# Three more seven-product quads in a fused attention and state-space block

## The chip, the cores and the metric

The kernel runs on one core of a Trainium2 chip. The metric is the device time of one execution in microseconds; the time given for a kernel is the median of its runs. One further execution is taken by the hardware profiler: its views are the page, groups of instructions, waits, the chain of waits that ended last, the order of time, and stretches (windows) with the busy time of every engine.

## The reference

One layer of a hybrid block on x of 256 rows and 2048 columns, all in float32:

```
proj = rms_norm(x) @ w_in            # q, k, v, z_a, z_s, xbc, dt, g_a, g_s
o_a  = dilated attention of q, k, v (16 heads, three patterns mixed) * silu(z_a)
y    = rms_norm(chunked state-space scan of xbc, dt * silu(z_s))
merged = sigmoid(g_a) * (o_a @ w_attn_branch) + sigmoid(g_s) * (y @ w_ssm_branch)
out  = rms_norm(x + merged @ w_out)
```

With 256 rows nearly all work is weight matrices streaming past a small x. The weights hold some 481 units of 128 x 1024 numbers (512 KB each).

## The kernel before, in words

**Units and their split.** A weight unit is loaded on SP's DMA queue into a ring of five buffers (`w`). ScalarE writes its high part `h` (line 278), VectorE the rest `l = w - h` (line 279), and TensorE multiplies with three matmuls of 512 columns each: x's high part with h and with l, x's low part with h (lines 484 to 486, in `triple`). That is how float32 accuracy is had from the faster matmul format. `h` and `l` have four buffers each.

**Passes.** The second half of the program runs in this order: state-space branch (`ssm`, two passes of 16 quads), value projection (`v`, two passes), 16 heads (`q`, `k`, `za` and the attention itself), attention gate (`ga`, two passes, units 385 and 401 on), attention branch (`attn`, units 417 and 433 on), output (`out`, units 449 and 465 on). A pass (function `gemm_pair`) makes 256 x 1024 outputs out of quads. A quad is two units of weights: two k blocks by two column blocks. It is done in one of two ways:

- plain: 2 k blocks x 2 row halves x 2 column halves, a `triple` each: 24 matmuls. VectorE and ScalarE split two units.
- seven-product (Strassen's scheme): seven triples, 21 matmuls. It needs sums of the weights: `t` (its sum made earlier and spilled to DRAM in `sum_jobs`, or made on the spot) and `u` (line 565), and sums of x (`sx`, made in `keep_left`, spilled, fetched back by `fetch_left`). VectorE makes `la`, `lc`, `ltt`, `ltu` and line 565, ScalarE `ha`, `hc`, `htt`, `htu`. `htt/ltt` and `htu/ltu` take two buffer pairs (`ht`, `lt`); the value passes have two pairs more.

`S_QUADS` lists the seven-product quads of each pass, `V_ORDERS`, `G_ORDERS`, `A_ORDERS` the order in which a pass takes its eight quads. After a pass, `fold` adds four product banks (two ScalarE copies, lines 589 and 590, and VectorE lines 591 to 594), then the element-wise sums follow (1018 for the gate, 1155 for the attention branch) and, for the attention branch, the merge with the gates (1144, 1145). The merged blocks are then transposed on TensorE (`turn_m`, line 1137, banks `mtp`). The two passes of a pair use the PSUM banks in swapped roles.

**What sets the order.** The order of quads and the hooks that start loads (`behind_unit`: a one-column GpSimd copy that waits for a unit's split, and a DMA on SP behind it) are written by hand. Between them a list scheduler places instructions on every engine; the splits of weights go ahead of other work by `L_AHEAD`. Each engine runs its own list strictly in order. Hooks sit on plain quads' units alone.

**Places.** `cst` holds in columns 0 to 384 the causal mask of the scan, then the identity, `ones` and `sel`; `cw` the convolution's weights. The attention's tables (distances and counts, 768 columns) have had a tile of their own, `dc`, in pool `xl`, loaded behind unit 274. Pool `xk` holds one `sx` tile, `xl` three, `vx` (in the value passes) one for quad 3.

Of the kernel before, what the change touches and what calls it, by code (L numbers as in the profile page):

```python
# [9 lines left out]
F32 = mybir.dt.float32  # L10
F32R = mybir.dt.float32r
# [4 lines left out]
P = 128  # L16
# [48 lines left out]
SUM_UNITS = 2, 9, 16  # L65
LEFT_EVERY, ATT_EVERY = 11, 4
SUM_LAG = 3
# [131 lines left out]
def hybrid_block(ctx: ExitStack, tc: tile.TileContext, wall, xt, x, pk_d, cst_d, fw_d, out):  # L199
# [34 lines left out]
    def behind_unit(n, f):  # L234
        on_unit.setdefault(n, []).append(f)
# [56 lines left out]
    def blocks(t, c):  # L292
        return [t[:, i, (c + j) * 512 : (c + j + 1) * 512] for i in range(2) for j in range(2)]
# [143 lines left out]
    def fetch_left(kept, pool, bufs, key, x, spare, u):  # L437
        def get(behind):
            sx = new_sx(pool, bufs, spare, f"{key[0]}{key[1]}")
            gp.tensor_copy(sx[:, 0, 0, 0:1], behind)  # L440
            nc.sync.dma_start(sx.bitcast(F32), lefts[key])
            kept[key[1]] = left_parts(sx, x, spare)

        behind_unit(u, get)
# [156 lines left out]
    def rsqrt_rows(sums, n, name):  # L601
        var = lead.tile([P, 2], F32, name=f"var_{name}", tag="var", bufs=1)
        ve.tensor_scalar(var, sums, 1.0 / n, EPS, ALU.mult, ALU.add)
        r = lead.tile([P, 2], F32, name=f"r_{name}", tag="rr", bufs=1)
        gp.tensor_tensor(r, var, half, ALU.pow)
        hr = lead.tile([P, 2], F32, name=f"hr_{name}", tag="hr", bufs=1)
        ve.tensor_scalar(hr, r, 0.5, None, ALU.mult)
        return r, hr
# [84 lines left out]
    with tc.tile_pool(name="ssm", bufs=2) as sp:  # L693
# [223 lines left out]

        for n, q in enumerate(SX_X + SX_V):
            behind_unit(begin + 3 + n * LEFT_EVERY, lambda behind, q=q: left_x(q, behind))
# [108 lines left out]
    with tc.tile_pool(name="vx", bufs=1) as vx:  # L1028
        tl = big.tile([P, 4, UNIT], F32R, name="tl_v", tag="yo0b")
        room["tl"] = [(tl[:, 2 * n], tl[:, 2 * n + 1]) for n in range(2)]  # L1030
        for n, q in enumerate(SX_V):
            fetch_left(sx_of_x, vx, len(SX_V), ("x", q), two_kts(XT, q), 0, FIRST[("v", 0)])
        for n, q in enumerate(SX_X[1:]):
            fetch_left(sx_of_x, xl, len(SX_X) - 1, ("x", q), two_kts(XT, q), 0, FIRST[("v", 0)] + 1 + n)
        for c in (0, 2):
            es, prods = gemm_pair(
                ("v", c), lambda kt: XT[:, kt, :], KT, sx_of_x, c == 2, order=V_ORDERS[c], room=room
            )
            dst = blocks(vt, c)
            fold(prods, dst)  # L1040
            for d, e in zip(dst, es):
                ve.tensor_tensor(d, e, d, ALU.add)
    sx_of_o = {}

    with tc.tile_pool(name="att", bufs=2) as ap:
# [4 lines left out]
        def scores(h, q, k, p):  # L1050
# [4 lines left out]
            slope = 2.0 ** (-8.0 * (h + 1) / NH)  # L1055
            ve.scalar_tensor_tensor(t, dist_c, slope / SCALE, sps[:, :384], ALU.mult, ALU.add)
            st = ap.tile([P, 8], F32, name=f"st{h}", tag="st", bufs=1)
# [6 lines left out]
            for i, (a, b) in enumerate(parts):  # L1064
                ve.scalar_tensor_tensor(
                    p[:, a:b], p[:, a:b], 1.0, count_c[:, a:b], ALU.mult, ALU.mult,
                    accum_out=st[:, 4 + i : 5 + i],
                )
# [10 lines left out]
        def mix(h, pT, za):  # L1079
# [13 lines left out]
        sum_jobs(  # L1093
            SUMS_ATT, range(FIRST[("q", 0)] + 7, N_UNITS, ATT_EVERY),
            [
# [188 lines left out]
```

## Time and profile before

| | us |
|---|---|
| median of 3 runs (lowest, highest) | 1381.28 (1380.21, 1382.47) |
| the profiled execution, in all | 1381.59 |
| its span, first to last instruction | 1379.8 |
| TensorE busy, VectorE busy, ScalarE busy, GpSimd busy | 1368.4, 1168.4, 836.6, 142.5 |

The span leaves out 1.8 us around the instructions. In the order of time a row is: start, duration, engine, line, operation, tile written <- tiles read, shape, count; what stands in brackets is idle time ahead of it and who ended it. A group's row has, behind the bar, busy time and mean of one, and behind the next bar the idle time ahead of it with its releasers. Tile names in the trace come without their numbers.

### The profile page before, as it was taken

To read this page: it belongs to the slowest core of one execution; us is meant where nothing else is said; L and a number is where in the kernel's file an instruction comes from. 1 tells how busy PE (TensorE), PEld (TensorE's weight loads), DVE (VectorE), ACT (ScalarE), POOL (GpSimd) and SP (SyncE) were. 2 spreads that over 40 slices of the span, in tenths; PEclk is the share of its full clock that TensorE was granted. 3 is DMA by queue.
4 is the path that set the end of the run, shared out by engine and by line. 5 is a ranking of instruction groups with operands and counts; after the bars stand their busy time and mean duration, and the time that the engine had idled before them with its cause. 6 is when DMAs were issued, how large, how long until landed. Compare 5 with 4: busy or idle time off the path is not lost.

```text
span 1379.8 us, 20706 instructions
## 1 busy us (share of the span) xinstructions
PE 1368.4 (99%) x7266; PEld 1166.4 (85%) x7266; DVE 1168.4 (85%) x1753; ACT 836.6 (61%) x1306; POOL 142.5 (10%) x226
## 2 busy tenths in 40 slices
PE   9999999999999999999999999999999999999997
PEld 7888888888888888888888888888888888888886
DVE  6897999897899898788989887777877788888997
ACT  7655777675667676666565554454445556655554
POOL 2301111101010100010001001211111000000112
PEclk9999999999999999999999999999999999999999
DMA  9766978778787867578677668888888757875773
GB/s 348 232 193 198 334 261 284 263 245 283 249 278 236 302 200 223 175 240 277 228 259 273 209 218 282 280 275 276 289 288 300 241 163 268 290 224 177 247 271 122
DMA packets 105080, 345.00 MB, mean 250 GB/s; under 512 B 11728, under 2 KB 13712, under 8 KB 104976
## 3 DMA queue, kind: packets, MB, share of 16 engines
q1 hardware_dynamic: 103536, 339.62, 73.7%
q10 hardware_dynamic: 1440, 4.06, 0.8%
q8 instruction: 57, 0.93, 0.3%
q14 instruction: 47, 0.39, 0.1%
HBM read 314.87 MB, written 28.77 MB: 249 GB/s over the span
## 4 chain that ended last, share of the span: by engine, by line
PE 95%; DMA 2%; ACT 1%; issue 1%; DVE 1%; SPq 0%; POOL 0%; POOLq 0%; ACTq 0%; DVEq 0%
PE ps_xs L333 8%; PE ps_zs L333 8%; PE ps_za L333 4%; PE ps_k L333 4%; PE ps_q L333 4%; PE ps_xs L339 4%; PE ps_zs L339 4%; PE ps_ssm L485 3%; PE ps_ssm L486 3%; PE ps_ssm L484 3%; PE ps_q L339 2%; PE ps_k L339 2%; PE ps_za L339 2%; PE ps_gs L421 2%; PE ps_gs L422 2%; PE ps_gs L420 2%
## 5 line engine op out<-in xcount | busy, mean ns | idle before, releaser
L278 ACT ACTIVATE h<-w 128x1024 fp32r<-128x1024 f32 (+1 forms) x398 | 413.8, 1047 | 303.9 <-issue 80.9
L279 DVE TENSOR_TENSOR l<-w,h 128x1024 fp32r<-128x1024 f32 (+1 forms) x398 | 478.8, 1209 | 114.0 <-ACT h L278 110.4
L333 PE MATMUL ps_zs<-XT,h 128*128 128x512 f32 x496 | 172.1, 393 | 0.0
L333 PE MATMUL ps_xs<-XT,h 128*128 128x512 f32 x496 | 171.6, 393 | 0.0
L339 PE MATMUL ps_zs<-XT,l 128*128 128x256 f32 x496 | 134.8, 280 | 0.9 <-DVE l L279 0.9
L339 PE MATMUL ps_xs<-XT,l 128*128 128x256 f32 x496 | 133.7, 277 | 0.0
L333 PEld LDWEIGHTS ps_xs<-XT,h 128*128 128x128 f32 x496 | 91.3, 188 | 19.4
L333 PEld LDWEIGHTS ps_zs<-XT,h 128*128 128x128 f32 x496 | 91.3, 188 | 18.8
L339 PEld LDWEIGHTS ps_zs<-XT,l 128*128 128x128 f32 x496 | 93.3, 188 | 3.7 <-DVE l L279 1.6
L339 PEld LDWEIGHTS ps_xs<-XT,l 128*128 128x128 f32 x496 | 93.2, 188 | 2.1
L333 PE MATMUL ps_q<-XT,h 128*128 128x512 f32 x256 | 91.1, 404 | 0.0
L333 PE MATMUL ps_k<-XT,h 128*128 128x512 f32 x256 | 88.6, 395 | 0.0
L333 PE MATMUL ps_za<-XT,h 128*128 128x512 f32 x256 | 88.4, 394 | 0.0
L551 ACT ACTIVATE ha<-wa 128x1024 fp32r<-128x1024 f32 x43 | 45.4, 1055 | 43.6 <-PE ps_ssm L486 12.9
L339 PE MATMUL ps_q<-XT,l 128*128 128x256 f32 x256 | 68.4, 278 | 0.0
L339 PE MATMUL ps_k<-XT,l 128*128 128x256 f32 x256 | 68.4, 277 | 0.0
L339 PE MATMUL ps_za<-XT,l 128*128 128x256 f32 x256 | 68.4, 277 | 0.0
L792 ACT ACTIVATE gt<-acb,acT 128x128 f32<-128x128 f32 x128 | 44.0, 391 | 28.8 <-DMA acb<-acum_d 27.4
L552 DVE TENSOR_TENSOR la<-wa,ha 128x1024 fp32r<-128x1024 f32 x43 | 52.4, 1219 | 9.3 <-ACT ha L551 9.2
L552 DVE TENSOR_TENSOR ltu<-wa,htu 128x1024 fp32r<-128x1024 f32 x38 | 46.3, 1219 | 15.9 <-ACT htu L551 15.9
L333 PEld LDWEIGHTS ps_k<-XT,h 128*128 128x128 f32 x256 | 47.0, 188 | 9.9
L333 PEld LDWEIGHTS ps_q<-XT,h 128*128 128x128 f32 x256 | 47.1, 188 | 9.7
(688 smaller groups left out, 3315.1 us busy)
## 6 DMA issues: line engine op xcount, KB each, us to landing
w<-in_wall SPq DMA_DIRECT2D x394, 512.0 KB, 4.8
wa<-in_wall SPq DMA_DIRECT2D x43, 512.0 KB, 5.1
th_a<-in_wall SPq DMA_DIRECT2D x19, 512.0 KB, 5.6
sums_at<-in_wall SPq DMA_DIRECT2D x18, 512.0 KB, 4.7
acb<-acum_d SPq DMA_DIRECT2D x32, 256.0 KB, 3.8
t_ssm<-sums_at SPq DMA_DIRECT2D x13, 512.0 KB, 4.8
wt<-t_ssm SPq DMA_DIRECT2D x13, 512.0 KB, 4.7
th_a<-in_wall SPq DMA_DIRECT2D x19, 256.0 KB, 6.2
```

What stands on the lines that cost most here:

```text
L278: ac.activation(h[:, a:b], w[:, a:b], AF.Copy)
L279: ve.tensor_tensor(l[:, a:b], w[:, a:b], h[:, a:b].bitcast(F32), ALU.subtract)
L333: high = pe.matmul(acc, h[:, kk, :], xs_of(kt), start=(kt == 0), stop=False)
L339: low = pe.matmul(acc[:, S:], l[:, kk, :], xs_of(kt)[:, :S], start=False, stop=(kt == KT - 1))
L420: pe.matmul(accs[i], xh, h[:, kk], start=(kt == 0), stop=False)
L421: pe.matmul(accs[i], xh, l[:, kk], start=False, stop=False)
L484: pe.matmul(acc, xh, h, start=start, stop=False)
L485: pe.matmul(acc, xh, l, start=False, stop=False)
L486: pe.matmul(acc, xl, h, start=False, stop=stop)
L551: ac.activation(h, src, AF.Copy)
L552: ve.tensor_tensor(l, src, h.bitcast(F32), ALU.subtract)
L792: ac.activation(g4[:, n, b], acb[:, j, b // 2 * P : b // 2 * P + P], AF.Relu, scale=-1.0, bias=sc[:, h : h + 1],)
```

## The change

Quad 3 becomes a seven-product quad in both gate passes, and quad 5 in the first attention pass. The gate's order takes quad 4 ahead of quad 1, so that plain quads are 0, 1 and 7; the first attention pass takes 5 ahead of 6. The left sums of x for quad 3, so far used in the first value pass alone, are kept through the gate: `xl` has four tiles, and `vx` goes. To make room, `dc` goes: the distances are loaded over the mask, the counts over `cw` and over `ones` and `sel`, by three loads. `rsqrt_rows` takes one tile instead of three. The sums to be made under the heads are 22 instead of 19, 3.75 units apart instead of 4, from the third unit on instead of the seventh.

```
-A_ORDERS = {0: (0, 1, 2, 4, 3, 6, 5, 7), 2: (0, 2, 1, 4, 3, 5, 6, 7)}
+A_ORDERS = {0: (0, 1, 2, 4, 3, 5, 6, 7), 2: (0, 2, 1, 4, 3, 5, 6, 7)}
-G_ORDERS = {c: (0, 2, 1, 4, 3, 5, 6, 7) for c in (0, 2)}
+G_ORDERS = {c: (0, 2, 4, 1, 3, 5, 6, 7) for c in (0, 2)}
...
-    ("v", 0): (2, 3, 4, 5, 6), ("v", 2): (2, 4, 5, 6), ("ga", 0): (2, 4, 5, 6), ("ga", 2): (2, 4, 5, 6),
-    ("attn", 0): (2, 4, 6), ("attn", 2): (2, 4, 5, 6), ("out", 0): (3, 5), ("out", 2): (3, 5),
+    ("v", 0): (2, 3, 4, 5, 6), ("v", 2): (2, 4, 5, 6), ("ga", 0): (2, 3, 4, 5, 6), ("ga", 2): (2, 3, 4, 5, 6),
+    ("attn", 0): (2, 4, 5, 6), ("attn", 2): (2, 4, 5, 6), ("out", 0): (3, 5), ("out", 2): (3, 5),
...
-SX_X = (2, 4, 5, 6)
-SX_V = (3,)
-O_BEHIND = 7, 14, 15, 17
+SX_X = (2, 4, 3, 5, 6)
+O_BEHIND = 3, 14, 15, 17
...
-    dc = xl.tile([P, 768], F32, name="dc", tag="dc")
-    dist_c, count_c = dc[:, :384], dc[:, 384:]
-    behind_unit(FIRST[("v", 2)] + 1, lambda behind: fetch(dc, cst_d[:, :768], behind))
+    count = lead.tile([P, P], F32, name="count", tag="cw"), cst[:, 512:768]
+    for n, (dst, a) in enumerate(((mask3, 0), (count[0], 384), (count[1], 512))):
+        behind_unit(FIRST[("v", 2)] + n, lambda behind, dst=dst, a=a: fetch(dst, cst_d[:, a : a + dst.shape[-1]], behind))
...
-            SUMS_ATT, range(FIRST[("q", 0)] + 7, N_UNITS, ATT_EVERY),
+            SUMS_ATT, [FIRST[("q", 0)] + 3 + n * 15 // 4 for n in range(len(SUMS_ATT))],
```

Lines of the changed kernel are one lower up to about line 600, two lower in the state-space part and five lower from the attention on. TensorE's list is nine matmuls shorter. What moves on VectorE is shown at two places; the first number in a tile's name is the weight unit (a seven-product quad goes by its first unit), the second only tells instances apart.

The first place is VectorE in the first gate pass, where the last head's attention ends (p15, oaTb and sxt_o6 are its leftovers; units 385 to 388 are quads 0 and 1, 389 and 393 are quads 2 and 4). Before:

```order
L1071 TENSOR_SCALAR p15_11472<-p15_11472,st15_11557 128x256
L279 TENSOR_TENSOR l387_11671<-w387_11668,h387_11670 128x1024
L288 TENSOR_TENSOR oaTb_10571<-za14_11294,oaTb_10571 128x256
L288 TENSOR_TENSOR sxt_o6_11537<-sxt_o6_11537 128x512
L279 TENSOR_TENSOR l388_11677<-w388_11674,h388_11676 128x1024
L552 TENSOR_TENSOR la393_11710<-wa393_11704,ha393_11709 128x1024
L552 TENSOR_TENSOR lc393_11714<-wc393_11706,hc393_11713 128x512
L565 TENSOR_TENSOR wa393_11704<-wa393_11704,th_a_7806 128x1024
L552 TENSOR_TENSOR ltu389_11638<-wa389_11619,htu389_11637 128x1024
```

The same place in the changed kernel:

```order
L1066 TENSOR_SCALAR p15_11495<-p15_11495,st15_11580 128x256
L551 TENSOR_TENSOR la393_11697<-wa393_11691,ha393_11696 128x1024
L287 TENSOR_TENSOR oaTb_10585<-za14_11317,oaTb_10585 128x256
L287 TENSOR_TENSOR sxt_o6_11560<-sxt_o6_11560 128x512
L564 TENSOR_TENSOR wa393_11691<-wa393_11691,th_a_7802 128x1024
L551 TENSOR_TENSOR lc393_11701<-wc393_11693,hc393_11700 128x512
L278 TENSOR_TENSOR l387_11737<-w387_11734,h387_11736 128x1024
L278 TENSOR_TENSOR l388_11743<-w388_11740,h388_11742 128x1024
L551 TENSOR_TENSOR ltu389_11661<-wa389_11642,htu389_11660 128x1024
```

Quad 4's la, lc and line 565's operation (now 564) have moved ahead of quad 1's two units.

The second place is VectorE at the end of attention pass 0 and the start of pass 2 (units 431 and 432 are quad 7 of pass 0, 429 its quad 6, 433 to 436 quads 0 and 1 of pass 2, 437 its quad 2; fin takes the fold, th_a and th_s the merge). Before:

```order
L279 TENSOR_TENSOR l431_12555<-w431_12552,h431_12554 128x1024
L279 TENSOR_TENSOR l432_12561<-w432_12558,h432_12560 128x1024
L592 TENSOR_TENSOR fin_12270<-pp_attn0_3_12353,fin_12270 128x512
L552 TENSOR_TENSOR ltt437_12693<-fin_12270,htt437_12692 128x1024
L593 TENSOR_TENSOR fin_12270<-fin_12270 128x512
L279 TENSOR_TENSOR l433_12642<-w433_12639,h433_12641 128x1024
L594 TENSOR_TENSOR fin_12270<-fin_12270 128x512
L279 TENSOR_TENSOR l434_12648<-w434_12645,h434_12647 128x1024
L1155 TENSOR_TENSOR fin_12270<-ps_attn0_0_12271,fin_12270 128x512
L1155 TENSOR_TENSOR fin_12270<-ps_attn0_1_12272,fin_12270 128x512
```

After them come, up to unit 435's l, 10 more operations of 512 columns, la437, line 565's on wa437, and lc437. The same place in the changed kernel:

```order
L278 TENSOR_TENSOR l432_12604<-w432_12601,h432_12603 128x1024
L551 TENSOR_TENSOR ltt429_12567<-fin_12307,htt429_12566 128x1024
L278 TENSOR_TENSOR l433_12685<-w433_12682,h433_12684 128x1024
L551 TENSOR_TENSOR ltu429_12571<-wa429_12553,htu429_12570 128x1024
L278 TENSOR_TENSOR l434_12691<-w434_12688,h434_12690 128x1024
L590 TENSOR_TENSOR fin_12307<-pp_attn0_2_12389,fin_12307 128x512
L1150 TENSOR_TENSOR fin_12307<-ps_attn0_0_12308,fin_12307 128x512
L591 TENSOR_TENSOR fin_12307<-pp_attn0_3_12390,fin_12307 128x512
L551 TENSOR_TENSOR ltt437_12736<-fin_12307,htt437_12735 128x1024
L1139 SCALAR_TENSOR_TENSOR th_a_7802<-th_a_7802,fin_12307 128x512
L592 TENSOR_TENSOR fin_12307<-fin_12307 128x512
L551 TENSOR_TENSOR la437_12727<-wa437_12722,ha437_12726 128x1024
```

Quad 6's ltt and ltu and all of the fold now stand behind unit 432's l; some of the merge has moved behind unit 435's l. Then follow 1140, 593, 1150, 564 on wa437, lc437, 1150 twice, 1139 and unit 435's l.

More of the change, by code (lines that the diff above doesn't have):

```diff
@@ L65 @@
 SUM_UNITS = 2, 9, 16
-LEFT_EVERY, ATT_EVERY = 11, 4
+LEFT_EVERY = 11
 SUM_LAG = 3
@@ L1023, in hybrid_block @@
     xl = ctx.enter_context(tc.tile_pool(name="xl", bufs=1))
[L1024 to L1026 removed]
+    count = lead.tile([P, P], F32, name="count", tag="cw"), cst[:, 512:768]
+    for n, (dst, a) in enumerate(((mask3, 0), (count[0], 384), (count[1], 512))):
+        behind_unit(FIRST[("v", 2)] + n, lambda behind, dst=dst, a=a: fetch(dst, cst_d[:, a : a + dst.shape[-1]], behind))
     room = room_of(big.tile([P, 6 * 512], F32, name="room_v", tag="yo0a"), 2, 2)
[L1028 to L1042, printed above, removed]
+    tl = big.tile([P, 4, UNIT], F32R, name="tl_v", tag="yo0b")
+    room["tl"] = [(tl[:, 2 * n], tl[:, 2 * n + 1]) for n in range(2)]
+    for n, q in enumerate(SX_X[1:]):
+        fetch_left(sx_of_x, xl, len(SX_X) - 1, ("x", q), two_kts(XT, q), 0, FIRST[("v", 0)] + n)
+    for c in (0, 2):
+        es, prods = gemm_pair(
+            ("v", c), lambda kt: XT[:, kt, :], KT, sx_of_x, c == 2, order=V_ORDERS[c], room=room
+        )
+        dst = blocks(vt, c)
+        fold(prods, dst)
+        for d, e in zip(dst, es):
+            ve.tensor_tensor(d, e, d, ALU.add)
     sx_of_o = {}
```

11 lines of the change are left out of this document (5 added, 6 removed).

## The prediction

> **What bounds the kernel now.** I read the page first, then the chain of waits, then stretches cut at the passes, then the order of time around the passes that change. From the page (40 slices of 34.5 us, busy tenths, and the granted TensorE clock):
>
> ```profile
> span 1379.8 us, 20706 instructions
> PE 1368.4 (99%) x7266; PEld 1166.4 (85%) x7266; DVE 1168.4 (85%) x1753; ACT 836.6 (61%) x1306; POOL 142.5 (10%) x226
> PE   9999999999999999999999999999999999999997
> PEclk9999999999999999999999999999999999999999
> PE 95%; DMA 2%; ACT 1%; issue 1%; DVE 1%; SPq 0%; POOL 0%; POOLq 0%; ACTq 0%; DVEq 0%
> ```
>
> TensorE sets the end: 95% of the chain is its work, and its clock is granted in full in every slice. A busy share alone does not prove that matmuls stand as close as they can, so the pitch comes next. Two rows of TensorE in the order of time, at the change from attention pass 0 to pass 2 (start, duration):
>
> ```profile
> 1242.38 0.39 PE L484 MATMUL ps_attn<-h,oaTa 128*128 128x512 f32 x1
> 1244.42 0.39 PE L484 MATMUL ps_attn<-h,oaTa 128*128 128x512 f32 x1
> ```
>
> The first and the tenth of ten matmuls in a row: nine steps in 2.04 us, 0.227 us each, although one lasts 0.39 (they overlap). Now the passes (PE, weight load, VectorE, ScalarE, GpSimd busy, clock, DMA share): the two value passes, the two gate passes, the two attention passes.
>
> ```profile
> 745.00:787.00 42.00, 42.00 (x187) 34.75 (x187) 37.98 (x41) 24.09 (x28) 3.29 (x3) 1.00 0.71 247
> 787.00:829.00 42.00, 42.00 (x191) 34.88 (x189) 38.30 (x41) 23.32 (x26) 0.00 (x0) 1.00 0.58 193
> 822.00:1117.00 295.00, 295.00 (x1719) 259.10 (x1718) 222.50 (x419) 146.03 (x224) 43.83 (x57) 1.00 0.81 273
> 1117.00:1159.00 42.00, 42.00 (x191) 34.76 (x190) 35.28 (x52) 25.64 (x33) 0.00 (x0) 1.00 0.68 221
> 1159.00:1201.00 42.00, 42.00 (x188) 34.84 (x187) 37.66 (x41) 27.14 (x33) 2.12 (x4) 1.00 0.82 289
> 1201.00:1243.00 42.00, 42.00 (x187) 34.80 (x186) 36.30 (x41) 24.20 (x28) 0.00 (x0) 1.00 0.73 230
> 1243.00:1286.00 43.00, 43.00 (x199) 35.63 (x199) 38.30 (x48) 24.26 (x31) 3.16 (x1) 1.00 0.58 186
> ```
>
> TensorE never waits in any of them: 187 matmuls in 42 us is the same 0.225 us pitch. So a matmul taken out is worth its pitch, and any wait that the change makes is paid in full. The runner-up is VectorE, with 4.3 to 6.7 us to spare in each pass that changes.
>
> **The matmuls removed.** A plain quad issues 2 x 2 x 2 x 3 = 24 matmuls of 512 columns, a seven-product quad 7 x 3 = 21. Three quads change: nine matmuls fewer, 9 x 0.227 = 2.04 us, all of it on the path. The Trainium skill ("TensorE: Matmul & The Clock Gate", section "Wait — 56ns, not 53.3ns?") gives 215.7 ns from start to start at 512 columns with a warm clock; by that estimate it would be 1.94 us. The trace's step is 5% longer, and the sum goes by the trace.
>
> **The work added on VectorE.** Rows at the start of attention pass 2:
>
> ```profile
> 1239.37 1.28 DVE L1155 TENSOR_TENSOR fin<-ps_attn,fin 128x512 f32<-128x512 f32 x2
> 1240.57 1.28 DVE L1144 SCALAR_TENSOR_TENSOR th_a<-th_a,fin 128x512 f32<-128x512 f32 x2
> 1249.45 2.35 DVE L279 TENSOR_TENSOR l<-w,h 128x1024 fp32r<-128x1024 f32 x2
> 1251.72 1.22 DVE L552 TENSOR_TENSOR ltu<-wa,htu 128x1024 fp32r<-128x1024 f32 x1
> ```
>
> Two operations of 1024 take 2.27 us from start to start, 1.135 each (the second is done 1.22 after its start); two of 512 take 1.20, 0.60 each. A plain quad costs VectorE 2 x 1.135 = 2.27; a seven-product quad with its sum made earlier 4 x 1.135 + 0.60 = 5.14. So each changed pass gets 2.87 us more for VectorE and becomes 0.68 shorter: 35.28, 37.66 and 36.30 turn into about 38.2, 40.5 and 39.2 of 41.3. It fits, but the lead over TensorE must be built up and used at the right places. Value pass 0 is the precedent: the same order with five such quads, 37.98 of 42, no wait; but it has four pairs of ht/lt buffers, the gate passes two.
>
> The sums of the three quads are made under the heads' projections: two operations of 0.60 each, 3.6 us in all, on a VectorE that is busy 222.5 of 295 us there, plus nine one-column GpSimd copies and their loads. Cost nothing; bounds 0 to 0.3 (half of one such operation arriving late), since the lead is largest there.
>
> **First gate pass: nothing, bounds 0 to 0.7.** Here the head's leftovers and the second seven-product quad meet. Before:
>
> ```profile
> 1119.82 0.39 PE L485 MATMUL ps_ga<-l,XT 128*128 128x512 f32 x1
> 1123.31 0.55 DVE L1071 TENSOR_SCALAR p<-p,st 128x128 f32<-128x128 f32 x2
> 1124.54 1.23 DVE L279 TENSOR_TENSOR l<-w,h 128x1024 fp32r<-128x1024 f32 x1 [0.69 <-ACT h L278]
> ```
>
> Now quad 4's la, wa and lc stand ahead of unit 387's l, with the two leftovers (0.34 and 0.60). From 1123.86 (end of the head's scaling): 2 x 1.135 + 0.94 + 0.60 + 1.22 puts that l at 1128.9. TensorE's new order first uses it 9.8 us after the matmul at 1119.82 (43 matmuls of 0.227), at 1129.6: margin 0.7. If VectorE again waits 0.69 for ScalarE, the margin is just gone.
>
> **Attention pass 0 to 2: 0.8 us lost.** Quads 5 and 6 now stand together ahead of plain quad 7, so VectorE still owes ltt and ltu of quad 6, the whole fold, and the merge when pass 2 begins. Before (unit 432's l is the second of the first row; unit 435's the first of the row at 1249.45 above):
>
> ```profile
> 1231.37 2.35 DVE L279 TENSOR_TENSOR l<-w,h 128x1024 fp32r<-128x1024 f32 x2
> 1238.07 0.62 PE L485 MATMUL ps_attn<-l,oaTb 128*128 128x512 f32 x2
> 1250.32 0.82 PE L1137 MATMUL mtp<-cst,th_s 128*128 128x128 f32 x6
> 1250.89 0.48 PE L485 MATMUL ps_attn<-lc,sx_o 128*128 128x512 f32 x1
> 1251.91 0.39 PE L485 MATMUL ps_attn<-l,oaTa 128*128 128x512 f32 x1
> ```
>
> Unit 432's l was made at 1233.72 and used at 1238.30, margin 4.58; unit 435's was made at 1250.67 and used at 1251.91, margin 1.24. VectorE had 16.5 us of rows between them (6 x 1.135 + 16 x 0.60) and took 16.95. In the new order it has 8 of 1024 and 12 of 512 there: 9.08 + 7.20 = 16.3, or 16.8 with the same 0.5 of waits. TensorE needs 55 matmuls and two transposes: 12.7. The margin shrinks by 3.6 to 4.1. Up to unit 439's l come 5 x 1.135 + 6 x 0.60 = 9.3 against 32 matmuls and 14 transposes (six in 0.57), 8.6: another 0.7. In all 4.3 to 4.8. The margin to start from is 4.58 as before, or that of a pass that ends 5, 6, 7, as the gate pass does:
>
> ```profile
> 1150.04 1.22 DVE L279 TENSOR_TENSOR l<-w,h 128x1024 fp32r<-128x1024 f32 x1
> 1154.88 0.39 PE L485 MATMUL ps_ga<-l,XT 128*128 128x512 f32 x1
> ```
>
> made 1151.26, used 1154.88: 3.62. The least margin that cost nothing is 0.38, at the end of value pass 2 (819.63 + 1.22 against 821.23):
>
> ```profile
> 819.63 1.22 DVE L279 TENSOR_TENSOR l<-w,h 128x1024 fp32r<-128x1024 f32 x1
> 821.23 0.39 PE L485 MATMUL ps_v<-l,XT 128*128 128x512 f32 x1
> ```
>
> So the wait is between 0.1 (4.58 - 4.3 = 0.3 left where 0.4 is needed) and 1.6 (3.62 - 4.8). I take the middle, 0.8. What pays it back later is nothing: TensorE is the path.
>
> **Moved loads.** The 384 KB of tables come as three loads instead of one, for places whose last readers are long done, at units 273 to 275 instead of 274; two more GpSimd copies and two more issues on SP's queue, ahead of weight loads.
>
> ```profile
> dc<-in_cst SPq DMA_DIRECT2D x1, 384.0 KB, 4.7
> POOL sx_o L440 <- ACT h L278: 120.6, 2, 109.2
> SPq L441 <- POOL sx_o L440: 5.0, 3, 2.3
> w<-in_wall SPq DMA_DIRECT2D x394, 512.0 KB, 4.8
> ```
>
> Same bytes at a DMA share of 0.58: nothing, at most 0.7. Quad 2's sx_o is now fetched behind unit 404 instead of 408. GpSimd has only later sx_o copies queued behind it; on SP, quad 5's wc and all later weights stand behind its load, and three such loads held SP for 5.0 us (2.3 at most) without a wait of TensorE. Nothing, at most 0.5, since a weight load lands 4.8 us after its issue and the ring holds five units. Where x's parts are made (quad 3 third instead of last) changes no count: nothing.
>
> **Sum.** The profiled execution took 1381.59 in all: 1381.59 - 2.04 + 0.8 = 1380.35. The median shown, 1381.28, is 0.31 lower: **1380.0 us**.
>
> **Rivals.** *The whole gain:* the start margin holds at 4.5 and VectorE has no waits; 1381.28 - 2.04 = 1379.2. For it: value pass 0 and the gate passes already run such orders without a hole. Chance 0.27.
>
> *No change:* both tight places are at their bad end (0.7 + 1.6 = 2.3); 1381.5. For it: VectorE at 40.5 of 41.3 leaves little to rebuild a margin. Chance 0.21.
>
> *Slower:* the two pairs of ht/lt buffers become the pace.
>
> ```profile
> L551 ACT ACTIVATE htu<-wa 128x1024 fp32r<-128x1024 f32 x15 | 15.8, 1055 | 11.7 <-PE ps_ga L486 6.3 <-DMA sxd_o<-sxt_o 3.0 <-DVE wa L565 1.6
> L552 DVE TENSOR_TENSOR ltu<-wa,htu 128x1024 fp32r<-128x1024 f32 x15 | 18.3, 1220 | 7.5 <-ACT htu L551 7.5
> ```
>
> Quad to quad, TensorE frees a pair, ScalarE refills it (1.06), VectorE too (1.22), while TensorE has 15 matmuls, 3.4 us. With one instruction more ahead in each queue (1.05 + 1.14) the trip takes 4.5 and TensorE waits 1.1. New neighbours are quads 2 and 4, and 3 and 5, in each gate pass, and 5 and 6 in attention pass 0: five times 1.1 is 5.4, and the end is 1384.6. It decides once a refill stands behind another instruction in both queues at most of these five. For it: ScalarE and VectorE do wait for this trip, 6.3 and 7.5 us. Against it: neighbours 5 and 6 of the gate passes cost TensorE nothing. Chance 0.06.
>
> The Trainium skill ("Perfetto Trace Analysis", section "Identifying the Most-Contended Engine") holds matmul busy time a poor measure and weighs weight-load share against the others' occupancy: here 85% and 85%, a tie. By it work moved to VectorE would win nothing, as in *no change*; the even pitch of 0.227 speaks against it.
>
> **How the numbers follow.** Forecast 0.46, whole gain 0.27, no change 0.21, slower 0.06. 0.2% is 2.76 us, about what a measurement of this kernel tells from no change; the three runs span 1380.21 to 1382.47. Below 1378.5 only the whole gain with a lucky median comes: a fifth of 0.27, and some of the forecast, 0.10 in all. Above 1384.0: the slower case and a little of no change, 0.07. Within: 0.83. The range runs from 1378.4 (whole gain less 0.8 of scatter) to 1382.6 (no change plus 1.1).
>
> **What would show it.** The page should count nine matmuls fewer. TensorE in the order of time should show its only new holes within some 10 us of the first transposes mtp, adding up to 0.8; margins of 0.5 to 1 at unit 387. No hole over 0.1 there: the whole gain. Holes at ltt and ltu throughout the gate passes: the buffer pairs. VectorE should be about 2.9 us busier in each changed pass. A difference that starts ahead of 745 us would make the working wrong altogether.

## The result and the profile after

The changed kernel takes 1390.77 us (median of 7 runs, 1386.46 to 1398.76), the kernel before 1382.04 in the same comparison (1380.21 to 1383.10): a ratio of 1.0065, with a 95% interval of 1.0047 to 1.0082. The forecast was 1380.0, the range ended at 1382.6. The change is slower, and its runs lie 12 us apart where those of before lie 3. The profiled execution took 1391.35. Four executions on record, one each of runs 4, 6 and 10 below and one of the kernel before, took 1954 to 1956 us at a granted clock of 0.65; the ratios leave them out, the medians given for these runs do not (without them 1387.13, 1385.42 and 1386.44).

From the page of the changed kernel (span and busy times, busy tenths of TensorE and its clock, shares of the chain of waits):

```profile
span 1389.5 us, 20759 instructions
PE 1371.0 (99%) x7257; PEld 1164.7 (84%) x7257; DVE 1181.6 (85%) x1768; ACT 840.9 (61%) x1312; POOL 146.5 (11%) x237
PE   9999999999999999999999999999999999999997
PEclk9999999999999999999999999999999999999999
PE 91%; issue 3%; DMA 2%; DVE 2%; ACT 1%; POOL 1%; SPq 0%; POOLq 0%; ACTq 0%; DVEq 0%
```

Nine matmuls fewer (7257 against 7266), and VectorE 13.2 us busier, close to the 12.2 that the prediction's prices give (3 x 2.87 + 3.6). The slices look the same, and the clock is full: nothing here shows the loss. The stretches cut at the passes do (same columns and same cuts as in the prediction; the last row is the first part of the output, which the prediction did not show):

```profile
1117.00:1159.00 42.00, 41.77 (x192) 34.38 (x191) 37.62 (x54) 27.21 (x36) 0.00 (x0) 1.00 0.68 222
1159.00:1201.00 42.00, 40.78 (x179) 32.83 (x177) 36.29 (x40) 25.49 (x31) 4.63 (x3) 1.00 0.74 249
1201.00:1243.00 42.00, 40.61 (x177) 33.09 (x178) 38.13 (x39) 27.94 (x33) 1.24 (x1) 1.00 0.74 252
1243.00:1286.00 43.00, 39.78 (x179) 31.66 (x178) 38.47 (x47) 22.03 (x27) 0.00 (x0) 1.00 0.53 178
1286.00:1330.00 44.00, 43.28 (x199) 35.57 (x198) 40.53 (x56) 24.34 (x31) 4.75 (x3) 1.00 0.76 266
```

The last of these rows in the kernel before:

```profile
1286.00:1330.00 44.00, 44.00 (x204) 36.50 (x203) 39.88 (x52) 25.22 (x31) 1.90 (x3) 1.00 0.82 285
```

TensorE, full in every row before, now stands in all five: 1243 to 1286 holds 179 matmuls where it held 199. In the order of time these are its waits of over 0.25 us (what stands in brackets is idle time ahead of the matmul, and who ended it):

```profile
1201.33 0.49 PE L483 MATMUL ps_attn<-h,oaTa 128*128 128x512 f32 x1 [1.33 <-ACT th_a L588]
1202.11 0.50 PE L484 MATMUL ps_attn<-l,oaTa 128*128 128x512 f32 x1 [0.28 <-DVE l L278]
1204.09 0.50 PE L483 MATMUL ps_attn<-h,oaTa 128*128 128x512 f32 x1 [0.78 <-ACT h L277]
...
1256.78 0.50 PE L484 MATMUL ps_attn<-l,oaTa 128*128 128x512 f32 x1 [1.60 <-DVE l L278]
1265.66 0.50 PE L483 MATMUL ps_attn<-hc,sx_o 128*128 128x512 f32 x1 [1.14 <-ACT hc L550]
1266.61 0.73 PE L483 MATMUL ps_attn<-h,oaTa 128*128 128x512 f32 x2 [0.44 <-ACT h L277]
...
1292.48 0.50 PE L483 MATMUL ps_out<-h,mT 128*128 128x512 f32 x1 [0.72 <-ACT fin L588]
```

Three places: the start of the attention branch, its change from pass 0 to 2, and the start of the output. A wait costs more than its idle time, since matmuls overlap and the first ones behind it are slower (0.50 instead of 0.39), so holes are counted here as the distance from start to start beyond the usual 0.227. Counted so: 3.2 us at the first place, 4.6 at the second, 1.0 at the third, and 1.3 in small pieces inside the gate passes: 10.1 in all.

That fits the clock. From the first matmul of the value passes to the first of the last block (ps_right) the kernel before took 624.96 us, the changed one 633.16: 8.20 more, where 10.1 of holes less 2.04 for the matmuls make 8.1. This stretch, "the second half" below, compares profiles better than whole times do: the first 745 us differ by -1.2 to +3.6 us from profile to profile of all kernels here, whichever part of the change they hold.

### The profile page after: what moved, and what is told of

Its sections match the earlier page's. It is cut to its first block, busy times and chain, and to the rows that moved or that the text cites. A ratio compares the mean times of both kernels' runs of the same rounds, so it can differ in the third digit from the quotient of the medians.

```text
span 1389.5 us, 20759 instructions
## 1 busy us (share of the span) xinstructions
PE 1371.0 (99%) x7257; PEld 1164.7 (84%) x7257; DVE 1181.6 (85%) x1768; ACT 840.9 (61%) x1312; POOL 146.5 (11%) x237
## 4 chain that ended last, share of the span: by engine, by line
PE 91%; issue 3%; DMA 2%; DVE 2%; ACT 1%; POOL 1%; SPq 0%; POOLq 0%; ACTq 0%; DVEq 0%
PE ps_zs L332 8%; PE ps_xs L332 8%; PE ps_za L332 4%; PE ps_k L332 4%; PE ps_q L332 4%; PE ps_zs L338 4%; PE ps_xs L338 4%; PE ps_ssm L484 3%; PE ps_ssm L485 3%; PE ps_ssm L483 3%; PE ps_q L338 2%; PE ps_k L338 2%; PE ps_za L338 2%; PE ps_gs L420 2%; PE ps_gs L421 2%
## 5 line engine op out<-in xcount | busy, mean ns | idle before, releaser
L277 ACT ACTIVATE h<-w 128x1024 fp32r<-128x1024 f32 (+1 forms) x392 | 407.9, 1048 | 305.3 <-issue 65.8
L278 DVE TENSOR_TENSOR l<-w,h 128x1024 fp32r<-128x1024 f32 (+1 forms) x392 | 472.3, 1210 | 108.7 <-ACT h L277 105.8
L550 ACT ACTIVATE ha<-wa 128x1024 fp32r<-128x1024 f32 x46 | 48.6, 1057 | 53.2 <-DMA wa<-in_wall 11.1
L551 DVE TENSOR_TENSOR la<-wa,ha 128x1024 fp32r<-128x1024 f32 x46 | 56.2, 1221 | 13.2 <-ACT ha L550 13.0
L551 DVE TENSOR_TENSOR ltu<-wa,htu 128x1024 fp32r<-128x1024 f32 x41 | 50.0, 1221 | 11.3 <-ACT htu L550 11.3
```

Source lines behind the costliest of these rows:

```text
L277: ac.activation(h[:, a:b], w[:, a:b], AF.Copy)
L278: ve.tensor_tensor(l[:, a:b], w[:, a:b], h[:, a:b].bitcast(F32), ALU.subtract)
L550: ac.activation(h, src, AF.Copy)
L551: ve.tensor_tensor(l, src, h.bitcast(F32), ALU.subtract)
```

## What held TensorE

**The start of the attention branch.** The chain of waits runs through a queue that the prediction had priced at nothing. Ahead of the weights of units 417 and on, SP's list has the load of a left sum (sx_o), and that load waits for a one-column GpSimd copy. GpSimd and SP in the order of time, changed kernel:

```profile
1190.69 4.45 POOL L439 CAST sx_o<-h 128x1 fp32r<-128x1 f32 x2 [13.30 <-ACT h L277]
```

```profile
1185.31 2.60 SPq L266 DMA_DIRECT2D w<-in_wall  x2
1195.05 0.33 SPq L440 DMA_DIRECT2D sx_o<-sxd_o  x1
1195.47 0.37 SPq L266 DMA_DIRECT2D w<-in_wall  x1
1195.90 0.42 SPq L440 DMA_DIRECT2D sx_o<-sxd_o  x1
1196.42 1.51 SPq L266 DMA_DIRECT2D w<-in_wall  x3
```

The first row covers two copies; the first of them alone lasts 4.33 us (the second 0.18). It wrote one column of 128 numbers. SP issued nothing from 1187.9 to 1195.05; the next weights landed at 1199.7 and 1203.0, and h, l and TensorE followed (line 588, for which the first matmul waits, is the fold's copy; it stands in ScalarE's list right behind unit 417's h). What VectorE did meanwhile:

```profile
1190.35 1.22 DVE L564 TENSOR_TENSOR wa<-wa,th_a 128x1024 f32<-128x1024 f32 x1
1191.48 1.22 DVE L278 TENSOR_TENSOR l<-w,h 128x1024 fp32r<-128x1024 f32 x1
1192.62 1.22 DVE L551 TENSOR_TENSOR ltu<-wa,htu 128x1024 fp32r<-128x1024 f32 x1
1193.75 1.22 DVE L278 TENSOR_TENSOR l<-w,h 128x1024 fp32r<-128x1024 f32 x1
1195.02 1.23 DVE L551 TENSOR_TENSOR ltt<-th_a,htt 128x1024 fp32r<-128x1024 f32 x1
1200.83 1.23 DVE L278 TENSOR_TENSOR l<-w,h 128x1024 fp32r<-128x1024 f32 x1 [4.58 <-ACT h L277]
```

Four operations one behind the other (each starts before the last has ended) and then a pause of 0.05 at 1194.97. The copy ended at 1195.02, in that pause. The Trainium skill ("SBUF — State Buffer", section "Who interferes with whom") says that a VectorE instruction with two SBUF inputs and a GpSimd instruction that reads SBUF share a port, and that the second to issue blocks until the first has finished. The trace agrees that it blocks, and shows more: this copy did not get in between operations that followed without a pause; it stood through three ends of operations.

The kernel before had all of this, at harmless places. Its GpSimd rows there, and one further on:

```profile
1188.67 1.24 POOL L440 CAST sx_o<-h 128x1 fp32r<-128x1 f32 x1 [11.37 <-ACT h L278]
1190.54 0.51 POOL L440 CAST sx_o<-h 128x1 fp32r<-128x1 f32 x1 [0.63 <-PE pp_ga L486]
...
1279.90 3.16 POOL L646 COPY fin<-h 128x1 f32<-128x1 f32 x1 [81.25 <-ACT h L278]
```

A copy that takes 0.18 us elsewhere took 1.24, 0.51 and 3.16. And its SP list had units 417 and 418 ahead of the loads of these two left sums (quads 4 and 5), so a late copy held up nothing that was due.

The first two rows also show that a copy does not always stand until VectorE pauses: VectorE ran without a pause from 1186.85 to 1193.28 there, and each of the two copies ended within 0.05 us of the end of a VectorE operation in the middle of that stretch (1189.87 and 1191.00). What decides whether a copy gets in there is not shown; runs 9 and 11 below have a pair that differs in little but the moment at which the copy began.

**From attention pass 0 to 2.** VectorE, ScalarE and SP in the changed kernel:

```profile
1244.76 0.69 DVE L590 TENSOR_TENSOR fin<-pp_attn,fin 128x512 f32<-128x512 f32 x1 [1.82 <-PE pp_attn L485]
```

```profile
1251.15 0.63 ACT L550 ACTIVATE hc<-fin 128x512 fp32r<-128x512 f32 x1 [3.05 <-DMA fin<-in_wall]
...
1264.98 0.63 ACT L550 ACTIVATE hc<-fin 128x512 fp32r<-128x512 f32 x1 [9.31 <-DMA fin<-in_wall]
```

```profile
1248.54 0.33 SPq L533 DMA_DIRECT2D fin<-in_wall  x1
...
1259.87 0.38 SPq L533 DMA_DIRECT2D fin<-in_wall  x1
```

VectorE was ahead and stood 1.82 us in front of the fold, because quad 6, now seventh of eight, had its last product at 1244.7. From unit 432's l (made 1238.40) to unit 435's (1256.72) it then took 18.3 us: the 16.3 that the prediction counted, the 1.82, and 0.2. The wc loads of pass 2 go into fin's first 512 columns (the row "wc" of `room`), where the fold and the merge of pass 0 still work; so each waits for a merge step, SP issues it at 1248.54 and 1259.87, and hc at the head of ScalarE's list holds the units behind it.

**The start of the output.** GpSimd and ScalarE:

```profile
1287.74 3.66 POOL L644 COPY fin<-h 128x1 f32<-128x1 f32 x1 [82.41 <-ACT h L277]
```

```profile
1291.43 0.35 ACTq L645 DMA_DIRECT2D fin<-in_x  x1
1291.83 0.60 ACT L588 ACTIVATE fin<-pp_attn 128x512 f32<-128x512 f32 x1 [3.00 <-POOL fin L644]
```

The same kind of copy again (3.16 in the kernel before, without harm). Here ScalarE issues the load itself, and its fold (line 588), for which the output's first matmul waits, stands behind it.

## The experiments

Theories: A, GpSimd copies that stand still hold a queue; B, the fold of attention pass 0 comes late, and loads with it; against them, that the moved tables and loads cost the time, that the holes are one chain, or that VectorE is simply too full.

**1. The moves alone.** The changed kernel with the quads and orders of before:

```
-    ("attn", 0): (2, 4, 5, 6) ... ("ga", 0): (2, 3, 4, 5, 6), ("ga", 2): (2, 3, 4, 5, 6)
+    ("attn", 0): (2, 4, 6) ... ("ga", 0): (2, 4, 5, 6), ("ga", 2): (2, 4, 5, 6)
-O_BEHIND = 3, 14, 15, 17
+O_BEHIND = 7, 14, 15, 17
```

> The tables, the four xl tiles, the earlier sums and the one tile in rsqrt_rows as in the changed kernel, but the quads and orders of before (no quad new, O_BEHIND 7, 14, 15, 17). Theory A (the loss is made by the new quads at the boundaries of passes): within 0.7 us of the kernel before, 1382.0, and no hole of TensorE over 0.3 us between 1117 us and the end. Rival B (the moves themselves delay the work: the changed kernel's trace is already 1.67 us late when the value passes begin): 1383.7 or more, the 1.67 us there at 745 us again.

Measured: 1381.36 against 1381.69, ratio 1.0002 (0.9994 to 1.0011), second half 0.37 longer, and no wait of TensorE in the list of waits between 1117 and 1300. The tables, the larger pool and the moved sums cost nothing that can be measured, and the late start of the changed kernel's profile does not come from them.

**2. The gate's quads alone** (first attention pass as before; O_BEHIND stays 3, 14, 15, 17).

> The changed kernel with the first attention pass as before (quads 2, 4, 6, order 0, 1, 2, 4, 3, 6, 5, 7): only the gate's two quads are new, six matmuls fewer. Theory A (each boundary has its own hole): -1.36 us for the matmuls, +3.4 at the change from gate pass 2 to the attention branch, +0.9 inside the gate passes: 1385.0; no hole at the change from attention pass 0 to 2. Rival (the holes are one chain, the first makes the lead so short that the second follows): holes at both places, 1389. What the prediction on record gave for these parts: 1380.7.

Measured: 1387.24, ratio 1.0042 (1.0030 to 1.0054), between the two. The second half is 7.45 longer, all of it at the start of the attention branch and before it (holes of 3.3, 0.5 and 1.3 us, and a stretch of slow matmuls behind them); from attention pass 0 to 2 there is none. So the places are separate, as A has it; the size was missed because the copy stood still for even longer here, and because of the clock. GpSimd and VectorE of this run:

```profile
1189.87 5.77 POOL L439 CAST sx_o<-h 128x1 fp32r<-128x1 f32 x2 [13.52 <-ACT h L277]
```

```profile
1189.72 1.22 DVE L564 TENSOR_TENSOR wa<-wa,th_a 128x1024 f32<-128x1024 f32 x1
...
1194.26 1.21 DVE L551 TENSOR_TENSOR ltt<-th_a,htt 128x1024 fp32r<-128x1024 f32 x1
1201.32 1.23 DVE L278 TENSOR_TENSOR l<-w,h 128x1024 fp32r<-128x1024 f32 x1 [5.84 <-ACT h L277]
```

Five operations without a pause end at 1195.47, and the first copy at 1195.52 (5.65 us).

The clock adds a second cost. In this profile the granted TensorE clock falls to 0.50 at 1203.45, behind the first two holes, and stays there for 6.8 us (a stretch, columns as before, and a matmul in it):

```profile
1206.00:1208.00 2.00, 2.00 (x6) 1.61 (x5) 2.00 (x4) 0.34 (x1) 0.22 (x1) 0.50 0.45 143
1206.41 0.63 PE L484 MATMUL ps_ga<-ltu,XT 128*128 128x512 f32 x1
```

From start to start a matmul takes 0.427 us there instead of 0.227, some 2.4 us in all. So a wait can cost more than itself. In the changed kernel's profile the clock is full behind its holes; of its seven runs the two longest, 1392.64 and 1398.76, are the two with a mean granted clock of 0.996 (0.998 or 0.999 in the others), so a part of their spread may be this.

**3. Attention quad 5 alone** (gate as before, O_BEHIND 7, 14, 15, 17).

> The changed kernel with the gate passes as before (quads 2, 4, 5, 6, order 0, 2, 1, 4, 3, 5, 6, 7, O_BEHIND 7, 14, 15, 17): only quad 5 of the first attention pass is new, three matmuls fewer. Theory A: -0.68 us, +4.1 at the change from attention pass 0 to 2 (VectorE stands 1.8 us ahead of the fold for quad 6's last product, and a wc load waits for the merge), +0.9 at the end of pass 2: 1386.3. The prediction on record: -0.68 + 0.8, 1382.1. Rival (the hole needs the short lead that the gate passes leave): 1382 to 1383.

Measured: 1385.51, ratio 1.0031 (1.0021 to 1.0041). The second half is 4.23 longer, and all holes over 0.2 us lie at the two last places: 3.5 us from pass 0 to 2, 0.9 at the output. The lead that the gate leaves has no part in it. The prediction's 0.8 is out.

**4. Left sums fetched later.**

```
-O_BEHIND = 3, 14, 15, 17
+O_BEHIND = 3, 16, 17, 18
```

> The changed kernel with O_BEHIND = 3, 16, 17, 18 in place of 3, 14, 15, 17: the left sums for attention quads 4, 5 and 6 are fetched behind units 417, 418 and 419, so that the loads of units 417 and 418 stand ahead of them on SP's queue. Theory A (the 3.0 us hole at the start of the attention branch comes from weight loads that stand behind a left sum's load, itself behind a GpSimd copy that took 4.3 us): the hole goes, 1387.8 where the changed kernel has 1390.8. Rival (VectorE is late there, or the two buffer pairs): the hole stays, 1390.8.

Measured: 1387.58, ratio 1.0047 (1.0035 to 1.0060). The holes at the start of the attention branch are gone but for one of 0.46, the other two places stay (3.7 and 0.9, holes over 0.2 counted; 4.1 and 0.9 in the changed kernel). It was the place in SP's queue.

**5. The copy on ScalarE**, with places and queue as in the changed kernel.

```
-            gp.tensor_copy(sx[:, 0, 0, 0:1], behind)
+            if key[0] == "o":
+                ac.activation(sx[:, 0, 0, 0:1], behind, AF.Copy)
+            else:
+                gp.tensor_copy(sx[:, 0, 0, 0:1], behind)
```

> The changed kernel; only the one-column copy that starts the load of an attention quad's left sums (sx_o) is made by ScalarE instead of GpSimd; places and order of the loads as in the changed kernel. Theory A1 (the GpSimd copy was ready to run and stood still for 4.3 us while VectorE ran one operation after the other): the load goes out within 1 us of unit 415's h instead of 4.4 us after it, the holes at the start of the attention branch (3.0 us in the profiled run of the changed kernel) shrink under 0.5: 1387.5. Rival A2 (the copy waits for the last reader of the place or of the buffer, whatever engine makes it): unchanged, 1390.8, with ScalarE standing there instead.

ScalarE and SP of this run:

```profile
1190.53 1.06 ACT L277 ACTIVATE h<-w 128x1024 fp32r<-128x1024 f32 x1 [1.51 <-DMA w<-in_wall]
1191.62 0.20 ACT L440 ACTIVATE sx_o<-h 128x1 fp32r<-128x1 f32 x1
```

```profile
1191.85 0.33 SPq L443 DMA_DIRECT2D sx_o<-sxd_o  x1
```

The load goes out 0.26 us after h instead of 4.4, and no hole over 0.25 us is left at this place. The second half is 4.13 longer instead of 8.20. The median, 1389.01, is 1.5 above the forecast; this profile has 3.6 us more in its first 745 us, where the edit does nothing, and I can't say how much of that its other runs have. (3.4 of them are there when the program is 29 us old, with the granted clock at 0.50 for 3.4 us from 11.8.) With 4, the cause at this place is shown: the same load in the same place costs nothing when GpSimd is not in the way.

**6. wc in a place of its own**, on top of 4.

```
+        wc_own = fp.tile([P, 2, 512], F32, name="wc_own", tag="wc_own", bufs=1)
-        room = {..., "wc": [fin[:, i, :512] for i in range(2)]}
+        room = {..., "wc": [wc_own[:, i] for i in range(2)]}
```

> The run with the later left sums (O_BEHIND = 3, 16, 17, 18; 1387.58), and the attention branch's wc in a tile of its own instead of fin's first 512 columns, where the fold and the merge of pass 0 also work. Theory B1 (the second hole after the change from attention pass 0 to 2 comes from the wc load of quad 4, which waits for the merge, and from hc waiting for it at the head of ScalarE's queue): the second hole (0.86 + 0.72 us) goes, the first (1.9) stays: 1386.0. Rival B2 (VectorE's backlog alone sets both): 1387.6.

Measured: 1385.78, ratio 1.0029 (1.0019 to 1.0038). The time is as B1 had it, the mechanism only half: the holes from pass 0 to 2 went from 3.7 to 2.6, and hc of quad 4 still stands 7.3 us at the head of ScalarE's list, now for a place that TensorE has not left.

**7. The last product earlier**, on top of 4 (wc in fin again).

```
-A_ORDERS = {0: (0, 1, 2, 4, 3, 5, 6, 7), ...}
+A_ORDERS = {0: (0, 1, 2, 4, 5, 6, 3, 7), ...}
```

> The run with the later left sums (1387.58), and the first attention pass in the order 0, 1, 2, 4, 5, 6, 3, 7: the same four seven-product quads, but two plain quads (3 and 7) at the end instead of one, so that the last product is done before VectorE comes to the fold. Theory B3 (VectorE stood 1.8 us ahead of line 590 for quad 6's last product, and the merge and the wc loads behind it came that much later): both holes go but for some tenths: 1384.5. Rival B2 (17 us of VectorE work between the last unit of pass 0 and unit 435 are too many wherever the last product stands): a hole of 1.5 or more stays, 1386.5.

Measured: 1383.68, ratio 1.0017 (1.0008 to 1.0026). VectorE no longer waits ahead of line 590, but it now stands 3.7 us ahead of an ltu, for ScalarE's htu, and the holes from pass 0 to 2 are 2.1 us. The time is below B3's, the holes are the rival's: what is left has another cause than the last product. The edit with one line is worth more than 6.

**8. All mends**: 4, 6, 7, and ScalarE makes the copies that start loads on its own queue.

```
     def fetch(dst, src, behind, queue=nc.sync):
-        gp.tensor_copy(dst[:, 0:1], behind)
+        if queue is nc.scalar:
+            ac.activation(dst[:, 0:1], behind, AF.Copy)
+        else:
+            gp.tensor_copy(dst[:, 0:1], behind)
```

> All of these mends in one: the later left sums, the order 0, 1, 2, 4, 5, 6, 3, 7, wc in a tile of its own, and the copies that start the loads on ScalarE's DMA queue (x for the output, its weights) made by ScalarE instead of GpSimd, since one of them took 3.7 us at the end of attention pass 2 and held ScalarE's queue (0.9 us hole). The three new quads stay. Theory A and B (the loss is these four waits): the nine matmuls' gain is left, 1382.0 - 2.0 = 1380.0, up to 0.5 more. Rival (VectorE, busy 40.5 of 41.3 us in a pass, makes new holes where the old ones go): 1383 or more.

Measured: 1383.92, ratio 1.0017 (1.0008 to 1.0025): no better than 7. The hole at the output is gone, which shows its cause; 2.1 us from pass 0 to 2 stay, and gate pass 2 has one of 0.9, about what the output gained. That one comes with the edit of 6: runs 6, 8, 10 and 13, the four with wc in a tile of its own, have a hole of 0.6 to 1.05 ahead of this ha, the other runs at most 0.4 (run 11 apart, see below). With the tile free from the start, the attention branch's two wc loads go out early, at 1169.62 and 1170.05 here, just ahead of the wa load for which this ha waits; wa then takes 5.6 us to land, 4.5 in run 7. (In runs 6, 8 and 13 an l of VectorE ends at the same moment; in run 10 this ha starts before that l has ended.) No run moves these loads alone. What VectorE waited for most between 1225 and 1275 us in this run:

```profile
DVE ltu L551 <- ACT htu L550: 2.6, 1, 2.6
```

Quads 4, 5 and 6 now stand in a row, and htu of the third waits for a buffer of the two ht/lt pairs; the fold stands behind that ltu in VectorE's list.

**9. The gate's quads, mended**: 2 with O_BEHIND = 3, 16, 17, 18.

> Only the gate's two quads are new (first attention pass as before), and the left sums of the attention branch are fetched later (O_BEHIND = 3, 16, 17, 18). The gate-only run had 1387.24, with holes of 5.5 us in all at the change to the attention branch. Theory A (that wait is all that the gate's quads cost): 1381.6 - 1.36 for six matmuls + 0.4 for small holes inside the gate passes = 1380.6. Rival (VectorE at 40.5 of 41.3 us leaves no lead at the end of gate pass 2, whatever the loads do): 1382 or more, with holes at l of units 417 and 418.

Measured: 1380.78 against 1381.62, ratio 0.9997 (0.9988 to 1.0005); the second half is 0.28 shorter. The list of waits of TensorE from 1117 to 1300 has one row:

```profile
PE pp_ga L483 <- ACT htu L550: 0.3, 1, 0.3
```

So the boundary was most of what these two quads cost; of the 1.36 us that they save, small holes in the gate passes take the most back. Kernel and kernel before can't be told apart.

**10 and 11. Spread quads, and a third pair.** 8 with another order; 8 with a third ht/lt pair (wc back in fin).

```
+A_ORDERS = {0: (0, 2, 4, 1, 5, 6, 3, 7), ...}        # 10
+        tl_h = xl.tile([P, 2, 4, P], F32R, name="tl_h", tag="sx0", bufs=len(SX_X) - 1)
+        tl_l = fp.tile([P, UNIT], F32R, name="tl_l", tag="tl_l", bufs=1)
```

> All mends, with the first attention pass in the order 0, 2, 4, 1, 5, 6, 3, 7: plain quad 1 stands between the seven-product quads 4 and 5. In the run with all mends (1383.92) VectorE stood 2.6 us ahead of quad 6's ltu and ScalarE 2.8 ahead of its htu, for a place that TensorE had not left; 2.1 us of holes followed. Theory C1 (three seven-product quads in a row outrun the two ht/lt pairs, and the fold behind ltu comes late for it): the wait at ltu goes and the holes shrink by about 1.5: 1382.4. Rival C2 (the fold and merge, 9.6 us of VectorE, simply don't fit between the last units of one pass and the first of the next): holes of about 2 us again, 1383.9.

> All mends and the order 0, 1, 2, 4, 5, 6, 3, 7, with a third ht/lt pair for the attention passes (in the fourth left-sum place, free by then, and 4 KB more); wc goes back into fin. Theory C1 (the two pairs): the waits at htu and ltu of quad 6 go, VectorE comes to the fold 2 to 3 us earlier, and the holes at the change from pass 0 to 2 shrink from 2.1 to about 0.5: 1382.4. Rival C2 (too much VectorE work between the passes): 1383.9. If wc's place in fin matters too, a hole at the second hc: up to 1 us more.

Run 10: median 1387.94, ratio 1.0032 (1.0014 to 1.0050), but in two groups: five runs at 1380.92 to 1383.02, five at 1389.44 to 1392.10, one between. All five of the upper group have a mean granted clock of 0.996, all five of the lower one 0.998 or 0.999. Its profile is of the lower group: the wait at ltu is gone, the holes from pass 0 to 2 are 1.2 us, the second half is 0.94 longer. Run 11: 1387.16, ratio 1.0034 (1.0021 to 1.0047), and its profile shows what the upper group may be. GpSimd and SP in gate pass 2 of run 11:

```profile
1175.99 5.18 POOL L439 CAST sx_o<-h 128x1 fp32r<-128x1 f32 x1 [102.03 <-PE pp_ga L485]
```

```profile
1174.87 0.33 SPq L532 DMA_DIRECT2D th_a<-t_ga  x1
1181.19 0.33 SPq L440 DMA_DIRECT2D sx_o<-sxd_o  x1
```

This is the copy for the first left sum, behind unit 404. In the profiles of the changed kernel and of runs 2, 4, 6, 7, 8 and 10 it takes 0.18 or 0.19 us; here 5.18, SP is held for 6 us, and 3 us of holes follow in gate pass 2. From pass 0 to 2 there are 3.8 more, and behind them the granted clock is 0.50 for 3.4 us from 1256.7; the second half is 8.05 longer, and all five runs have a mean clock of 0.996 or 0.997. In run 9 the same copy meets the same six operations of VectorE (la, lc, ltu, line 564, ltt, la), the first five without a pause:

```profile
1174.68 1.24 POOL L439 CAST sx_o<-h 128x1 fp32r<-128x1 f32 x1 [112.06 <-ACT ha L550]
```

It began 0.03 us after the first of them and ended with it; in run 11 it began 0.10 after and stood until the pause behind the fifth. With so much lost elsewhere, run 11 tells nothing on the third pair.

**12. Both together.**

> The third ht/lt pair and the order 0, 2, 4, 1, 5, 6, 3, 7 together, wc in fin. Theory C1: no wait at ltu in pass 0, VectorE at the fold as early as it can be: 1381.5, the lowest of the runs with all three quads. Rival C2: 1383.5, since the same 17 us of VectorE work stand between the last unit of pass 0 and unit 435.

Measured: 1384.05, ratio 1.0018 (1.0010 to 1.0027). The holes from pass 0 to 2 are down to 0.9 (3.7 in run 4, 2.1 in 8, 1.2 in 10, holes over 0.2 counted). With every step beyond the usual counted, from 1243 to 1275 us, it is 1.6 here and 1.5 in run 10 (2.6 in 8). So C1 holds for about 1 us of these holes, and the third pair (with wc back in fin) adds nothing to the spread quads. The time is the rival's: 0.55 at the output is new, and this profile started 1.25 late.

**13 to 15. GpSimd out of the left sums' loads**, in 10, 9 and 12, by the edit of 5.

> The run with spread quads (order 0, 2, 4, 1, 5, 6, 3, 7 and all mends), with the copies that start the loads of the attention's left sums on ScalarE instead of GpSimd. Theory A (whether the GpSimd copy falls into a pause of VectorE is left to chance, and a miss holds SP's queue 4 to 6 us): one group of times, the upper one at 1389 to 1392 gone, median 1381.5. Rival (the two groups come from something else, TensorE's start or DMA): two groups again, median between 1384 and 1388.

> The run with the gate's two quads alone and later left sums (1380.78, three of eleven runs at 1382.7 to 1383.9), with these copies on ScalarE. Theory A: the runs at 1383 go, median 1380.3 (1381.6 - 1.36). Rival (the gate's quads leave small holes of VectorE's making): 1380.8 as it was.

> The run with the third pair and spread quads (1384.05), with these copies on ScalarE. Theory A and C1: what is left are holes of 0.6 us at the change from attention pass 0 to 2, so 1381.6 - 2.04 + 0.9 = 1380.5. Rival (VectorE is too short for three quads): 1383 or more.

Run 13: 1382.67, one group from 1381.54 to 1383.70, ratio 1.0006 (0.9997 to 1.0015). The upper group of run 10 is gone, and its low clocks with it (0.998 or 0.999 in all eleven runs); the copies are all that was changed in the program. The two ran on different chips, but runs 9 and 12, on the chip of run 10, have no mean clock below 0.998 either. The median is 1.2 over the forecast; 0.9 us of holes in gate pass 2 (ahead of an ha) and 1.3 from pass 0 to 2 remain. Run 14: 1381.06, ratio 0.9996 (0.9987 to 1.0005), with runs up to 1383.88 as in 9: not told apart from 9, so those runs had another cause. Run 15: 1384.09 (1383.35 to 1385.41), ratio 1.0019 (1.0010 to 1.0028): the rival's time. Its profile has 0.9 us of holes from pass 0 to 2 and 1.2 at the output, and a start 1.25 late; whether VectorE's load or the third pair's effect on the order makes it slower than 13 is open.

## Why the prediction was wrong

- **The matmuls removed** and **the work added on VectorE**: right (nine fewer; 13.2 us against 12.2). A slip in the working, 6 x 1.135 + 16 x 0.60, is 16.4, not 16.5; nothing rests on it.
- **First gate pass**: right. Unit 387's l was made at 1131.25 and used at 1131.85, a margin of 0.6 (0.5 to 1 was named); no wait there.
- **Moved loads**, the step that failed first. Of the tables it was right (run 1). Of the left sums it said that three such loads "held SP for 5.0 us (2.3 at most) without a wait of TensorE" and took nothing, at most 0.5. It looked at the load of quad 2 alone and did not follow those of quads 4 and 5, though the changed kernel's SP list has them ahead of units 417 and 418. In the changed kernel SP stood 7.2 us for one of them: 3.2 us of holes. In run 2 it stood 8.3, and 5.2 us of holes and 2.4 of the halved clock followed. What it had wrong is the wait: it priced a load that waits for a GpSimd copy by what such loads had cost at other places, and asked neither how long the copy can stand nor which weights are due behind it.
- **Attention pass 0 to 2**: right place, wrong size and an incomplete path. 0.8 was taken, 1.6 the upper bound; 4.6 came. VectorE's work was counted rightly (16.3 us of 18.3), the margin at the start was just under the range (3.44, with 3.62 to 4.58 named), but two things were not in the sum: the wait of 1.82 for the last product, and the wc loads that wait for the merge (run 6: about half of what they were charged with). Runs 7 and 10 together bear on the first: with the last product earlier and the quads spread, 1.2 us of holes over 0.2 are left. That VectorE simply has too much to do there for part of it, as rival C2 has it, is not ruled out.
- **The output** was not named at all. The 3.16 us copy of before was in the trace as a sign (run 8).
- **The slower rival** named the ht/lt pairs as the pace of all five neighbourings. They cost something once, with three quads in a row (runs 8, 10, 12: about 1 us), and some tenths at htu in the gate passes; they were not what made the change slow.
- **"any wait that the change makes is paid in full"** is too little: the first matmul behind a wait takes 0.50 us instead of 0.39 and the step behind it is 0.11 longer, and in runs 2 and 11 the clock was halved behind the holes.
- **The sign ahead of 745 us** that would have made the whole working wrong did show: the changed kernel's profile is 1.7 us late there. Run 1, with all that was moved into that part, is 0.7 early, and run 9, with the gate's quads, 1.0 early; so this is put down to differences between executions.

The forecast's outcome, the nine matmuls' gain less 0.8, was not reached by any version: the best with all three quads (run 13) is level with the kernel before, and the gate's two alone (9 and 14) can't be told from it.

## What to carry to other kernels

A change that fills the last idle time of an engine is also a change for all who need its pauses: look for small instructions that already take many times their shortest duration (0.18 against 1.24 and 3.16 here), and ask what queue stands behind them. When a load moves, follow each load that its hook list holds, and name what is due behind it on the same queue. When a step moves toward the end of a pass, count not only the work of the engine that takes over but when its first input is ready, and which loads go into the place where it still writes. And price a long wait of TensorE at more than its length: the clock behind it can be lower.

## What was not expected of the hardware

A GpSimd copy of one column stood still while VectorE ran four or five SBUF operations without a pause between them, 4.33, 5.65 and 5.18 us, and ended within 0.06 us of VectorE's first pause; the same copy on ScalarE took 0.20. Other copies got in at the end of one operation while VectorE ran on (1.24 us in the kernel before and in run 9). That VectorE is what such a copy waits for rests on these times and on run 5; no run changes VectorE's operations alone. The same copy ahead of the same operations took 1.24 us in run 9 and 5.18 in run 11; that it can go either way in executions of one program was not seen in two profiles, but runs 10, 11 and 13 together point to it, with two groups of times some 8 us apart that became one.

The granted clock fell to 0.50 behind holes in the profiles of run 2 (for 6.8 us) and run 11 (for 3.4 us) and did not in the changed kernel's, whose longest single hole was shorter (1.9 us, against 3.3 and 2.4).

The first 745 us of the program differ by up to 4.8 us between profiles, without relation to what was changed. In these profiles the differences arise before 29 us and between 118 and 164 us for the most part; why was left open.
